# MLP weight sums by accumulating DMAs between DRAM tensors instead of on VectorE

## The chip, the cores and the metric

The kernel runs on one NeuronCore of a Trainium2 chip. Its engines are named as the profile names them: PE (TensorE matmuls), PEld (the weight loads of PE), DVE (VectorE), ACT (ScalarE), POOL (GpSimd) and SP (SyncE, which here only issues DMAs). POOL also issues some DMAs. Sixteen DMA engines move the data of all queues. The metric is the time of one execution on the device in microseconds (us); the kernel before takes 2281.39 us, the median of 3 runs (2279.77 to 2282.05).

## The reference

One layer of a hybrid encoder over 2048 prompt frames and 64 frames of a running stream, 2112 tokens of width 1024, all in float32:

```python
a = rmsnorm(h, norm1);  z = a @ w_in                     # one projection, 2816 columns
attn_o = windowed attention with sinks;  ret_o = chunkwise retention
h = h + concat(attn_o, gated_norm(ret_o)) @ w_out
u = relu(rmsnorm(h, norm2) @ w_up)                       # 1024 x 4096
h = h + (u * u) @ w_down                                 # 4096 x 1024
y = rmsnorm(h, norm_f)
```

The change concerns `w_up` and `w_down`. Every matrix product is made from operands split into a high and a low part, three passes on TensorE. The two products of the MLP are moreover made by a seven-product (Strassen-Winograd) form: each matrix is cut into 2 x 2 blocks, and of the weight blocks L11, L12, L21 and L22 four sums and differences S1 to S4 are needed besides three blocks that are used as they are. They are the same for all tokens, so they are made once and kept in DRAM.

## The kernel before

The program has two stretches. The **first** (to about 800 us) runs over 17 tiles of 128 tokens (the last one has 64) and over two halves of the heads, `ph` 0 and 1: 34 tiles, the first and last of each half in pairs. A tile has three groups, `ci` 0 to 2, of 24 matmuls with 384, 512 and 512 columns, which make the projection z (lines 526 to 529). Between these matmuls stand the small matmuls of attention and retention of the tiles before: scores `s`, transposes `pt`, products `po`, and for retention `ptr`, `pss`, `pr` and `pst`. Where they stand is set by a planner written in the kernel (lines 474 to 511: latencies in `LAT`, a clock that counts the z matmuls). The order on PE and SP is the order of the code (`manual_schedule`); on DVE, ACT and POOL a scheduler sets it. Each engine works in its order and waits at an instruction whose semaphores have not come.

A tile needs a load of x (`xr`, line 142, one buffer), a load of the rotary table (`rt`, line 160, two buffers, so it waits until the rotation before has read its table) and in `ph` 0 a load of the tokens for the norm (`xk`, line 163). They are issued on SP. ACT and POOL split x into `xh` and `xl` (lines 153 and 154). DVE makes the three products of a rotation (lines 193 to 195), POOL adds them into `zr` or `qk` (line 196). POOL also makes `es` (line 290), a small sum that ACT exponentiates (line 291) for the softmax sum, and issues the stores of the mixed heads (`mscr`, lines 332 and 417).

The sums S1 to S4 are made beside this, in 64 units of 128 x 1024 numbers, one per group: `sum_load` (line 567) issues two loads of 256 KB each into a buffer `sr`, `sum_make` (line 583) makes the four results on DVE in four instructions of 128 x 256 (lines 587 to 590), `sum_store` (line 593) stores them with one DMA of 512 KB to `uscr` (of `w_up`) or `sscr` (of `w_down`). Units 0 to 32 lie in `ph` 0 from its third tile on, units 33 to 63 in `ph` 1 from its third tile on; the change from one half to the other has none. Loads, sums and stores of different units overlap through the four buffers of the pool `wraw`, which the raw weights of the projection use too.

The **second** stretch makes the output projection and the MLP. It reads `uscr` and `sscr` again and again (`upr`, line 845; `dr`, line 928). `up_pair` (line 853) adds the seven products into four results, `right_sums` (line 694) makes the sums of the right-hand operand, and a long loop adds the products of `w_down` into the residual.

Of the kernel before, what the change touches and what calls it, by code (L numbers as in the profile page):

```python
# [11 lines left out]
F32 = mybir.dt.float32  # L12
F32R = mybir.dt.float32r
AF = mybir.ActivationFunctionType
ALU = mybir.AluOpType
# [14 lines left out]
NB = 352  # L30
# [9 lines left out]
def body(ctx, tc, xt, xtok, w1, wout, wup, wdn, gains, sinks, ck, cv, sret, rot, rdec, qdec, dmask,  # L40
         yT, nkp, nvp, nrp, nks, nvs, nrs):
    nc = tc.nc
# [52 lines left out]
    pp = ctx.enter_context(tc.tile_pool(name="pp", bufs=5, space=PS))  # L95

    tabs = {}

    def load_tables(ph):
        h = slice(2 * ph, 2 * ph + 2)  # L100
# [79 lines left out]
    def rotate(dst, z, T, t, nb, hd, cs):  # L180

        h = hd // 2
        r = rs[:T, t:t + 1]
        t1 = wk.tile([128, 512], F32, name="rot1", tag="rot1", bufs=2)[:T, :nb * hd].rearrange(
            "p (b d) -> p b d", d=hd)
        t2 = wk.tile([128, 512], F32, name="rot2", tag="rot2", bufs=2)[:T, :nb * hd].rearrange(
            "p (b d) -> p b d", d=hd)
        c, s = cs[:, 0], cs[:, 1]

        def bc(a, w):  # L190
            return a.unsqueeze(1).broadcast_to([T, nb, w])
# [3 lines left out]
        nc.vector.scalar_tensor_tensor(t2[:, :, h:], z[:, :, :h], r, bc(s[:, h:], h), op0=ALU.mult, op1=ALU.mult)  # L195
        nc.gpsimd.tensor_add(dst, t1, t2)

    def new_kw():
        return wk.tile([128, 2, 256], F32R, name="kw", bufs=2)
# [342 lines left out]
    S = NT - 1  # L542
# [8 lines left out]
    a, b = tiles[:2]  # L551
# [12 lines left out]
    ws[0, 2] = load_w(0, 2)  # L564
    raws = None

    def sum_load(u):

        w, j, h = u // 32, u % 32 // 2, u % 2
        r = wraw.tile([128, 4, 256], F32, name="sr", tag="raw")  # L570
        if w == 0:
            c = slice(h * 256, h * 256 + 256)
            src = [wup[e].rearrange("p (a c) -> p a c", a=2)[:, :, c] for e in (j, j + 16)]
            dst = uscr[:, j, :, c]
        else:
            d, c = j // 4, slice((j % 4 * 2 + h) * 256, (j % 4 * 2 + h) * 256 + 256)
            src = [wdn[e].rearrange("p (a f) n -> p a (f n)", a=2)[:, :, c] for e in (d, d + 4)]
            dst = sscr[:, d, :, c]
        for k in range(2):
            nc.sync.dma_start(r[:, 2 * k:2 * k + 2], src[k])  # L580
        return r, dst

    def sum_make(r, dst):

        s = wraw.tile([128, 4, 256], F32, name="st", tag="raw")
        L11, L12, L21, L22 = (r[:, k] for k in range(4))
        nc.vector.tensor_add(s[:, 0], L21, L22)
        nc.vector.tensor_sub(s[:, 2], L11, L21)
        nc.vector.tensor_sub(s[:, 1], s[:, 0], L11)
        nc.vector.tensor_sub(s[:, 3], L12, s[:, 1])  # L590
        return s, dst

    def sum_store(s, dst):
        nc.sync.dma_start(dst.rearrange("s p c -> p s c"), s)

    todo, loaded, made = list(range(64)), [], []
    first, change = groups.index((0, 2, 0)), groups.index((0, S - 2, 0)) - 3
# [31 lines left out]
    assert not todo and not loaded and not made  # L629
    while queue:  # L630
        run_ready(1e9)
    nc.sync.dma_start(nks[0:64], ck[64:128])
# [217 lines left out]
    def up_pair(p, j, after):  # L850
# [5 lines left out]
        for i in ORDER:  # L856
            w = wslot("wu")
            split(w[:, 0], w[:, 1], src[i])
            ah, al = A[p, i]
            o = bank[i][:, :NB]  # L860
            for k in range(4):
                wh, wl = (w[:, x, k * 128:k * 128 + 128] for x in range(2))
                nc.tensor.matmul(o, wh, ah[:, k], start=k == 0 and i in (1, 6, 5), stop=False, skip_group_check=True)  # L863
                nc.tensor.matmul(o, wh, al[:, k], start=False, stop=False, skip_group_check=True)  # L864
                nc.tensor.matmul(o, wl, ah[:, k], start=False, stop=k == 3 and i in (2, 4, 3), skip_group_check=True)  # L865
            if i == 1:
                nc.scalar.activation(pc, o, AF.Copy)
            elif i == 6:
                add(u2, o, pc)
            elif i == 7:  # L870
                add(u3, o, pc)
                add(C[:, 3], c[:, :NB], u3)
            elif i == 2:
                nc.scalar.activation(C[:, 0], o, AF.Copy)
            elif i == 4:
                add(C[:, 2], o, pc)
            elif i == 3:
                add(C[:, 1], o, u2)
            after(i)
        V = C[:, 0:4]  # L880
        nc.scalar.activation(V, V, AF.Relu)
# [133 lines left out]
    for n, (p, i, d) in enumerate(steps):  # L1015
# [21 lines left out]
        if i == 1:  # L1037
            nc.scalar.activation(x1, o, AF.Copy)
            add(h[11], h[11], x1)
        elif i == 2:  # L1040
            add(h[11], o, h[11])
            s1(h[11])
        elif i == 6:
            add(x1, o, x1)
        elif i == 7:
            add(u3, o, x1)
            add(h[21], h[21], u3)
            add(h[22], h[22], u3)
        elif i == 4:
            add(h[21], o, h[21])  # L1050
            s1(h[21])
        elif i == 5:
            add(h[22], o, h[22])
            add(x1, o, x1)
# [109 lines left out]
```

## Time and profile before

| | before |
|---|---|
| median of 3 runs | 2281.39 us |
| the profiled execution's own time | 2280.28 us |
| its span, from the first to the last instruction | 2278.5 us |
| mean granted TensorE clock | 0.990 |
| PE / PEld / DVE / ACT / POOL busy | 97% / 93% / 69% / 49% / 19% |
| chain that ended last | PE 81%, DMA 6%, DVE 5%, POOL 2%, issue 2%, SPq 1%, ACT 1% |
| HBM read / written | 377.64 MB / 135.99 MB |
| DMA issued by SP (queue q1) | 503.77 MB, 67.2% of 16 engines' span |
| DMA issued by POOL (queue q0) | 9.87 MB, 1.3% of 16 engines' span |

Busy PE time is the union of matmul records whose ends are modelled, so a high share does not say that PE runs at its peak. The chain of waits follows the work that ended last back to what released it; a share of it is time in which only that step could move the end. "SPq", "DVEq" and the like are the sequencers of the engines, that is, the issue of DMAs and waits on semaphores.

### The profile page before, as it was taken

To read this page: it belongs to the slowest core of one execution; us is meant where nothing else is said; L and a number is where in the kernel's file an instruction comes from. 1 tells how busy PE (TensorE), PEld (TensorE's weight loads), DVE (VectorE), ACT (ScalarE), POOL (GpSimd) and SP (SyncE) were. 2 spreads that over 40 slices of the span, in tenths; PEclk is the share of its full clock that TensorE was granted. 3 is DMA by queue.
4 is the path that set the end of the run, shared out by engine and by line. 5 is a ranking of instruction groups with operands and counts; after the bars stand their busy time and mean duration, and the time that the engine had idled before them with its cause. 6 is when DMAs were issued, how large, how long until landed. Compare 5 with 4: busy or idle time off the path is not lost.

```text
span 2278.5 us, 35972 instructions
## 1 busy us (share of the span) xinstructions
PE 2216.6 (97%) x13256; PEld 2112.0 (93%) x13256; DVE 1571.3 (69%) x2716; ACT 1112.8 (49%) x1982; POOL 425.4 (19%) x518
## 2 busy tenths in 40 slices
PE   7999999999999999999999999999999999999998
PEld 5788888887888799999999999999999999999998
DVE  5777767576655647788678768666666876687665
ACT  5344446343343542455565657555544454454452
POOL 5444444333333222200000000000000200120012
PEclk9999999999999899999999999999999999999999
DMA  6666754577732579669879869776966777677662
GB/s 203 183 208 207 216 152 136 149 183 170 192 99 77 196 233 319 220 219 361 278 267 353 281 234 322 239 238 236 328 228 227 278 282 242 228 270 275 235 212 79
DMA packets 296753, 515.94 MB, mean 226 GB/s; under 512 B 23376, under 2 KB 194576, under 8 KB 296576
## 3 DMA queue, kind: packets, MB, share of 16 engines
q1 hardware_dynamic: 292608, 503.77, 67.2%
q0 software_dynamic: 3968, 9.87, 1.3%
q8 instruction: 104, 1.70, 0.3%
q14 instruction: 73, 0.60, 0.1%
HBM read 377.64 MB, written 135.99 MB: 225 GB/s over the span
## 4 chain that ended last, share of the span: by engine, by line
PE 81%; DMA 6%; DVE 5%; POOL 2%; issue 2%; SPq 1%; ACT 1%; DVEq 0%; POOLq 0%; ACTq 0%
PE y L1033 10%; PE y L1034 10%; PE y L1032 9%; PE b L864 4%; PE b L865 4%; PE b L863 4%; PE z L526 4%; PE z L527 4%; PE z L529 4%; PE y L738 3%; PE y L739 3%; PE y L740 3%; PE a L864 3%; PE c L864 3%; PE a L865 3%; PE c L865 3%
## 5 line engine op out<-in xcount | busy, mean ns | idle before, releaser
L1033 PE MATMUL y<-vl,wd 128*128 128x352 f32 x1344 | 438.2, 326 | 0.0
L1034 PE MATMUL y<-vh,wd 128*128 128x352 f32 x1344 | 436.1, 324 | 1.3 <-DVE wd L663 1.3
L1032 PE MATMUL y<-vh,wd 128*128 128x352 f32 x1344 | 433.6, 323 | 2.8 <-ACT wd L662 2.8
L526 PE MATMUL z<-w,xh 128*128 128x512 f32 (+1 forms) x816 | 326.8, 400 | 7.1 <-ACT w L86 7.1
L527 PE MATMUL z<-w,xh 128*128 128x512 f32 (+1 forms) x816 | 310.8, 381 | 1.3 <-DVE w L87 1.3
L662 ACT ACTIVATE wd<-dr 128x1024 fp32r<-128x1024 f32 x168 | 177.1, 1056 | 259.0 <-PE y L1034 189.6
L983 POOL TENSOR_TENSOR acc<-acc,sq 128x352 f32<-128x352 f32 x41 | 72.5, 1768 | 1222.4 <-ACT sq L979 1222.4
L662 ACT ACTIVATE wu<-upr 128x512 fp32r<-128x512 f32 x336 | 209.1, 627 | 174.5 <-PE b L865 83.7
L529 PE MATMUL z<-w,xl 128*128 128x512 f32 (+1 forms) x768 | 288.9, 376 | 0.0
L663 DVE TENSOR_TENSOR wd<-dr,wd 128x1024 fp32r<-128x1024 f32 x168 | 209.2, 1247 | 110.9 <-ACT wd L662 108.2
L663 DVE TENSOR_TENSOR wu<-upr,wu 128x512 fp32r<-128x512 f32 x336 | 230.8, 693 | 69.6 <-ACT wu L662 55.4
L1032 PEld LDWEIGHTS y<-vh,wd 128*128 128x128 f32 x1344 | 254.7, 189 | 3.1 <-ACT wd L662 3.1
L1034 PEld LDWEIGHTS y<-vh,wd 128*128 128x128 f32 x1344 | 253.2, 188 | 1.6 <-DVE wd L663 1.6
L1033 PEld LDWEIGHTS y<-vl,wd 128*128 128x128 f32 x1344 | 252.8, 188 | 0.0
L864 PE MATMUL b<-al,wu 128*128 128x352 f32 x576 | 185.8, 323 | 0.0
L863 PE MATMUL b<-ah,wu 128*128 128x352 f32 x576 | 185.6, 322 | 0.0
L865 PE MATMUL b<-ah,wu 128*128 128x352 f32 x576 | 185.4, 323 | 0.0
L526 PEld LDWEIGHTS z<-w,xh 128*128 128x128 f32 x816 | 156.7, 192 | 25.5 <-ACT w L86 7.3
L527 PEld LDWEIGHTS z<-w,xh 128*128 128x128 f32 x816 | 156.5, 192 | 22.6 <-DVE w L87 4.6
L529 PEld LDWEIGHTS z<-w,xl 128*128 128x128 f32 x768 | 144.8, 189 | 23.1
L663 DVE TENSOR_TENSOR vl<-rv,vh 128x1408 fp32r<-128x1408 f32 x84 | 136.2, 1623 | 37.8 <-ACT vh L662 37.3
L662 ACT ACTIVATE vh<-rv 128x1408 fp32r<-128x1408 f32 x84 | 116.0, 1380 | 55.5 <-DMA rv<-vscr 35.2
(283 smaller groups left out, 4835.6 us busy)
## 6 DMA issues: line engine op xcount, KB each, us to landing
rv<-vscr SPq DMA_DIRECT2D x84, 704.0 KB, 5.4
vscr<-C SPq DMA_DIRECT2D x48, 1056.0 KB, 5.9
upr<-uscr SPq DMA_DIRECT2D x192, 256.0 KB, 5.2
dr<-sscr SPq DMA_DIRECT2D x96, 512.0 KB, 4.4
upr<-in_wup SPq DMA_DIRECT2D x144, 256.0 KB, 4.2
dr<-in_wdn SPq DMA_DIRECT2D x72, 512.0 KB, 4.9
sr<-in_wup SPq DMA_DIRECT2D x64, 256.0 KB, 5.5
uscr<-st SPq DMA_DIRECT2D x32, 512.0 KB, 5.5
```

Source lines behind the costliest of these rows:

```text
L526: nc.tensor.matmul(z[:, :n], xh[:, k], wh, start=k == 0, stop=False)
L527: nc.tensor.matmul(z[:, :n], xh[:, k], wl, start=False, stop=k == NK - 1 and xl is None)
L529: nc.tensor.matmul(z[:, :n], xl[:, k], wh, start=False, stop=k == NK - 1)
L662: nc.scalar.activation(h, x, AF.Copy)
L663: sub(l, x, h.bitcast(F32))
L863: nc.tensor.matmul(o, wh, ah[:, k], start=k == 0 and i in (1, 6, 5), stop=False, skip_group_check=True)
L864: nc.tensor.matmul(o, wh, al[:, k], start=False, stop=False, skip_group_check=True)
L865: nc.tensor.matmul(o, wl, ah[:, k], start=False, stop=k == 3 and i in (2, 4, 3), skip_group_check=True)
L983: nc.gpsimd.tensor_add(self.acc, self.acc, sq)
L1032: nc.tensor.matmul(o, wh, vh, start=f == 0, stop=False)
L1033: nc.tensor.matmul(o, wh, vl, start=False, stop=False)
L1034: nc.tensor.matmul(o, wl, vh, start=False, stop=f == 15)
```

## The change

The 64 units on DVE go, with their loads, their stores and their buffers. There are 16 units of 2 MB instead, 8 of `w_up` and 8 of `w_down`, whose blocks are 512 KB each, and each unit is made by eight DMAs from DRAM to DRAM in six steps:

| step | on SP: plain copies | on POOL: accumulating DMAs |
|---|---|---|
| 0 | S1 = L21, S3 = L11 | |
| 1 | | S1 += L22, S3 += L21 |
| 2 | S2 = S1 | |
| 3 | | S2 += L11 |
| 4 | S4 = S2 | |
| 5 | | S4 += L12 |

Each step waits for the one before. Step k of unit u stands behind group `first + 4u + 2k`, so steps of three units meet in one place: every fourth group four copies are issued on SP, and two groups later four accumulating DMAs on POOL. On POOL they are ordered behind the last rotation addition traced before them (`last_pool`). The sums differ in sign from those before (additions only), so `right_sums` and some additions behind the products of the MLP become subtractions and the other way round, of the same shapes and in the same number.

```diff
@@ rotate
-        nc.gpsimd.tensor_add(dst, t1, t2)
+        last_pool[0] = nc.gpsimd.tensor_add(dst, t1, t2)
@@ instead of sum_load, sum_make, sum_store
-        for k in range(2):
-            nc.sync.dma_start(r[:, 2 * k:2 * k + 2], src[k])
...
-        nc.vector.tensor_add(s[:, 0], L21, L22)
-        nc.vector.tensor_sub(s[:, 2], L11, L21)
-        nc.vector.tensor_sub(s[:, 1], s[:, 0], L11)
-        nc.vector.tensor_sub(s[:, 3], L12, s[:, 1])
...
-        nc.sync.dma_start(dst.rearrange("s p c -> p s c"), s)
+    def blocks(u):
+        if u < 8:
+            j = slice(2 * u, 2 * u + 2), slice(2 * u + 16, 2 * u + 18)
+            return [uscr[k, j[0]].rearrange("j p c -> p j c") for k in range(4)], \
+                [wup[e, :, c:c + 512].rearrange("j p c -> p j c") for e in j for c in (0, 512)]
+        d, c = (u - 8) // 2, (u - 8) % 2 * 1024
+        return [sscr[k, d, :, c:c + 1024] for k in range(4)], \
+            [wdn[e].rearrange("p f n -> p (f n)")[:, a + c:a + c + 1024] for e in (d, d + 4) for a in (0, 2048)]
+
+    def sum_step(u, k):
+        (S1, S2, S3, S4), (L11, L12, L21, L22) = blocks(u)
+        copies, sums = {0: ([(S1, L21), (S3, L11)], ()), 1: ((), [(S1, L22), (S3, L21)]), 2: ([(S2, S1)], ()),
+                        3: ((), [(S2, L11)]), 4: ([(S4, S2)], ()), 5: ((), [(S4, L12)])}[k]
+        for dst, src in copies:
+            nc.sync.dma_start(dst, src)
+        with tc.issue_after(last_pool[0].ins):
+            for dst, src in sums:
+                nc.gpsimd.dma_start(dst, src, accum_op=ALU.add, max_dma_last_dim=4096)
+
+    first = groups.index((0, 2, 0))
+    for u in range(16):
+        for k in range(6):
+            sums.setdefault(first + 4 * u + 2 * k, []).append((u, k))
@@ in the loop over groups
-        if made:
-            sum_store(*made.pop())
-        if todo and (first <= i < change or ph == 1 and t > 1):
-            loaded.append(sum_load(todo.pop(0)))
...
         group(ph, t, ci, n_)
-        if loaded and (len(loaded) > 1 or not todo or not first <= i < change - 1 and ph == 0):
-            made.append(sum_make(*loaded.pop(0)))
+        for x in sums.pop(i, ()):
+            sum_step(*x)
@@ right_sums, and likewise behind the products
-        sub(t[:, 0:2], r[:, 1::2], r[:, 0:2])
-        sub(t[:, 2], r[:, 3], t[:, 0])
+        sub(t[:, 0:2], r[:, 0:2], r[:, 1::2])
+        add(t[:, 2], r[:, 3], t[:, 0])
```

On SP, one tile of `ph` 1 before (xr is the load of x, rt that of the rotary table, sr the loads of a unit, sscr<-st its store):

```order
L142 DMA xr<-in_xt 128x8x128 [waits DMAHW5_49,Pool_49]
L594 DMA sscr<-st 128x4x256 [waits DMAHW6_49,DVE_49]
L580 DMA sr<-in_wdn 128x2x256 [waits DMAHW2_49]
L580 DMA sr<-in_wdn 128x2x256 [waits DMAHW0_49]
L160 DMA rt<-in_rot 128x384 [waits DMAHW1_49,DVE_49]
L594 DMA sscr<-st 128x4x256
L580 DMA sr<-in_wdn 128x2x256 [waits DMAHW4_49,DMAHW3_49]
L580 DMA sr<-in_wdn 128x2x256
L594 DMA sscr<-st 128x4x256 [waits DMAHW5_49,DVE_49]
L580 DMA sr<-in_wdn 128x2x256 [waits DMAHW6_49,DMAHW2_49]
L580 DMA sr<-in_wdn 128x2x256 [waits DMAHW7_49]
L142 DMA xr<-in_xt 128x8x128 [waits DMAHW0_49,Pool_49]
```

Between the two loads of x stood two or three units; a store there waits for DVE. The same queue now, likewise in `ph` 1 (sscr<-sscr are the copies S4 = S2 and S2 = S1, which wait for accumulating DMAs, the semaphores DMASW; sscr<-in_wdn are S1 = L21 and S3 = L11):

```order
L143 DMA xr<-in_xt 128x8x128 [waits DMAHW6_49,DMAHW0_49,Pool_49]
L161 DMA rt<-in_rot 128x384 [waits DMAHW7_49,DVE_49]
L585 DMA sscr<-sscr 128x1024 [waits DMASW1_49]
L585 DMA sscr<-sscr 128x1024 [waits DMAHW1_49,DMASW2_49]
L585 DMA sscr<-in_wdn 128x1024 [waits DMAHW2_49]
L585 DMA sscr<-in_wdn 128x1024 [waits DMAHW3_49]
L143 DMA xr<-in_xt 128x8x128 [waits DMAHW6_49,DMAHW4_49,Pool_49]
L161 DMA rt<-in_rot 128x384 [waits DMAHW5_49,DVE_49]
L143 DMA xr<-in_xt 128x8x128 [waits DMAHW4_49,Pool_49]
```

No DMA of SP waits for a sum on DVE any more; the copies come four at a time, and two of the four wait for POOL's DMAs. On POOL, a place in `ph` 1 now (qk is the rotation addition of line 196, now 197, es the small sum for the softmax, now line 291, xl the split of x):

```order
L197 TENSOR_TENSOR qk<-rot_5784,rot_5785 128x512 [waits DVE_49]
L588 DMA sscr<-in_wdn 128x1024 [waits DMAHW7_49,DMASW6_49]
L588 DMA sscr<-in_wdn 128x1024 [waits DMAHW0_49,DMASW7_49]
L588 DMA sscr<-in_wdn 128x1024 [waits DMAHW1_49,DMASW0_49]
L588 DMA sscr<-in_wdn 128x1024 [waits DMAHW2_49,DMASW1_49]
L291 TENSOR_TENSOR es<-sk,ngm 128x4 [waits DVE_49]
L155 TENSOR_TENSOR xl<-xr,xh 128x1024 [waits DMAHW4_49,PE_49,Activation_49]
```

The four L588 rows are new, each behind the copy that it adds to (DMAHW); before, es stood right behind qk. The rest of POOL's order is nearly the same, and so is PE's. The 64 of them stand in 18 bursts of one to four, twelve of them behind a qk (ten of three or four, two of one or two) and six behind a zr. DVE has 256 instructions fewer.

More of the change, by code (lines that the diff above doesn't have):

```diff
@@ L97, in body @@
     tabs = {}
+    last_pool = [None]
     def load_tables(ph):
@@ L565, in body @@
     raws = None
[L567 to L578, printed above, removed]
-        for k in range(2):
-            nc.sync.dma_start(r[:, 2 * k:2 * k + 2], src[k])
-        return r, dst
@@ L583, in sum_make @@
[L583 to L593, printed above, removed]
-        nc.sync.dma_start(dst.rearrange("s p c -> p s c"), s)
-    todo, loaded, made = list(range(64)), [], []
@@ L597, in body @@
-    first, change = groups.index((0, 2, 0)), groups.index((0, S - 2, 0)) - 3
+    def blocks(u):
[6 more added lines that the diff above has]
+            [wdn[e].rearrange("p f n -> p (f n)")[:, a + c:a + c + 1024] for e in (d, d + 4) for a in (0, 2048)]
@@ L598, in body @@
+    first = groups.index((0, 2, 0))
+    sums = {}
+    for u in range(16):
+        for k in range(6):
+            sums.setdefault(first + 4 * u + 2 * k, []).append((u, k))
     aux = []
@@ L628, in body @@
             raws = None
-    assert not todo and not loaded and not made
+    assert not sums
     while queue:
@@ L868, in up_pair @@
             elif i == 6:
-                add(u2, o, pc)
+                sub(u2, o, pc)
             elif i == 7:
-                add(u3, o, pc)
-                add(C[:, 3], c[:, :NB], u3)
+                sub(u3, o, pc)
+                sub(C[:, 3], u3, c[:, :NB])
             elif i == 2:
@@ L875, in up_pair @@
             elif i == 4:
-                add(C[:, 2], o, pc)
+                sub(C[:, 2], o, pc)
             elif i == 3:
-                add(C[:, 1], o, u2)
+                sub(C[:, 1], o, u2)
             after(i)
@@ L1043, in body @@
         elif i == 6:
-            add(x1, o, x1)
+            sub(x1, o, x1)
         elif i == 7:
@@ L1052, in body @@
         elif i == 5:
-            add(h[22], o, h[22])
-            add(x1, o, x1)
+            sub(h[22], h[22], o)
+            sub(x1, o, x1)
             add(h[12], h[12], x1)
```

## The prediction

> **What bounds the kernel now.** I read the page first, then busy time by stage, then the waits of the first stretch, then its chain of waits in order of time.
>
> ```profile
> span 2278.5 us, 35972 instructions
> PE 2216.6 (97%) x13256; PEld 2112.0 (93%) x13256; DVE 1571.3 (69%) x2716; ACT 1112.8 (49%) x1982; POOL 425.4 (19%) x518
> ```
>
> PE is busy nearly throughout, so only time in which PE waits can be won. By stage (the stretch, its length, then busy time of PE, PEld, DVE, ACT, POOL with instruction counts, granted clock, DMA share and GB/s):
>
> ```profile
> 57.20:323.50 266.30, 254.14 (x1428) 218.44 (x1427) 196.01 (x491) 113.52 (x353) 113.92 (x184) 1.00 0.64 198
> 323.50:428.80 105.30, 104.67 (x591) 91.91 (x590) 67.22 (x159) 55.85 (x155) 43.74 (x63) 1.00 0.39 120
> 428.80:659.40 230.60, 215.86 (x1202) 186.72 (x1202) 159.16 (x422) 86.83 (x278) 77.62 (x103) 0.99 0.70 181
> 659.40:722.40 63.00, 63.00 (x362) 55.47 (x361) 32.43 (x87) 26.03 (x82) 22.54 (x30) 1.00 0.16 43
> 800.00:2278.50 1478.50, 1463.58 (x9102) 1462.57 (x9100) 1036.83 (x1391) 757.84 (x945) 114.53 (x66) 0.99 0.75 257
> ```
>
> I cut where the retention scores pss start; there are four per tile, so their counts in the first three stages give the tiles:
>
> ```profile
> L370 PE MATMUL pss<-rqT,rkT x48: 270/275/377, 57.2 to 301.8; 128*128 128x128 f32 x48
> ...
> L370 PE MATMUL pss<-rqT,rkT x20: 270/275/377, 323.5 to 417.3; 128*128 128x128 f32 x20
> ...
> L370 PE MATMUL pss<-rqT,rkT x40: 270/275/377, 428.8 to 636.9; 128*128 128x128 f32 x40
> ```
>
> Stage one, with sums: 12 tiles in 266.3 us, 22.2 us each. Stage two, the change of head groups, nearly without sums: 5 in 105.3, 21.06. Stage three, with sums: 10 in 230.6, 23.06. Stage four, without sums and with PE busy for all of its 63.0 us: three tiles, 21.0. So 21.0 us is PE's own pace, and tiles with sums take 1.2 and 2.06 us more. The MLP (last row) has PE busy for 99% of its time.
>
> The waits of the first stretch, and a piece of the chain in stage three, say why:
>
> ```profile
> DVE st L587 <- DMA sr<-in_wdn: 35.0, 13, 4.7
> DVE st L587 <- DMA sr<-in_wup: 22.5, 10, 4.0
> ...
> PE pr L380 <- DVE sd L373: 7.9, 6, 1.5
> ```
>
> ```profile
> 564.91 6.29 DMA sr<-in_wdn
> ...
> 571.30 0.68 DVE st L587
> ...
> 572.31 0.35 DVE sd L373
> ...
> 572.79 0.46 PE pr L380 x2
> ...
> 585.75 0.40 DVE rot L195
> ...
> 586.17 0.35 SPq L160
> ...
> 587.09 0.55 SPq L580
> ...
> 587.69 6.12 DMA sr<-in_wdn
> ```
>
> It is a ring. DVE stands at the sums until their load lands; the retention mask sd is queued behind them, PE waits for it (1.5 us at a time), the tile ends later, the rotation reads its table later, SP's load of the table, which waits for that, is later, and the next sum load stands behind it. From 564.91 to 587.69 the ring takes 22.78 us; without the sums PE's 21.0 us would decide.
>
> **What the change removes.** These instructions on DVE, with their waits:
>
> ```profile
> L588 DVE TENSOR_TENSOR st<-sr 128x256 f32<-128x256 f32 x64 | 43.5, 680 | 0.0
> ...
> L587 DVE TENSOR_TENSOR st<-sr 128x256 f32<-128x256 f32 x64 | 39.3, 614 | 58.8 <-DMA sr<-in_wdn 35.0 <-DMA sr<-in_wup 22.5 <-issue 1.3
> ...
> L589 DVE TENSOR_TENSOR st<-st,sr 128x256 f32<-128x256 f32 x64 | 30.4, 474 | 0.0
> ...
> L590 DVE TENSOR_TENSOR st<-sr,st 128x256 f32<-128x256 f32 x64 | 29.2, 456 | 0.8
> ```
>
> 142 us of DVE and 58 us of its waiting, in a stretch where DVE isn't the bound (159 of 230 us busy). What counts is the ring: 266.3 - 12 x 21.0 = 14.3 us in stage one and 230.6 - 10 x 21.0 = 20.6 in stage three, 34.9 at most. At least, if only the waits that name sd were won, 7.9. The ring was seen closed in nearly every tile of stage three: I take 20 there. In stage one the tiles also carry the load of the tokens and the first weights: I take 11 of 14. **Gain 31.**
>
> **What the signs cost.** Additions become subtractions of the same shape and number; the four rows above are an addition and three subtractions, and their means don't sort by operation. They lie beside a PE that is busy for 99%. Nothing; if a subtraction were a tenth slower, DVE (1036.83 of 1478.5 us) would still cover it.
>
> **What it adds on POOL.** 64 accumulating DMAs in 18 bursts of up to four. No row shows one. The nearest are POOL's stores of 256 rows (mix) and of 128 rows (st):
>
> ```profile
> L332 POOL DMA_DIRECT2D mscr<-mix x34 | 25.8, 760 | 39.1 <-DVE mix L331 28.2 <-ACT qT L246 3.8 <-PE pss L370 3.2
> ...
> L404 POOL DMA_DIRECT2D out<-st x8 | 4.6, 575 | 9.3 <-DVE st L401 9.3
> ```
>
> The blocks of w_up have 256 rows, those of w_down 128: four take 3.0 or 2.3 us. From above: if each row needed twice the work, the slope between the rows (185 ns per 128 rows) gives 1.13 us each, 4.5 a burst. Nothing would be the lower end. What stands behind a burst, in a tile of stage four:
>
> ```profile
> 680.73 0.42 PE L526 MATMUL z<-w,xh 128*128 128x384 f32 x1
> ...
> 683.89 0.55 SPq L142 DMA_DIRECT2D xr<-in_xt  x1
> ...
> 689.01 0.87 POOL L196 TENSOR_TENSOR zr<-rot,rot 128x320 f32<-128x320 f32 x1 [2.79 <-DVE rot L195]
> ...
> 696.55 0.35 SPq L160 DMA_DIRECT2D rt<-in_rot  x1
> ...
> 696.61 1.29 POOL L196 TENSOR_TENSOR qk<-rot,rot 128x512 f32<-128x512 f32 x1 [4.35 <-DVE rot L195]
> 698.07 0.20 POOL L290 TENSOR_TENSOR es<-sk,ngm 128x4 f32<-128x4 f32 x1 [0.17 <-DVE ngm L284]
> ...
> 699.61 0.21 ACT L291 ACTIVATE es<-es 128x4 f32<-128x4 f32 x1
> 699.94 0.39 ACT L364 ACTIVATE rkT<-ptr 128x256 f32<-128x256 f32 x1
> ...
> 701.37 0.60 PE L370 MATMUL pss<-rqT,rkT 128*128 128x128 f32 x4
> ```
>
> Behind zr POOL has 6.7 us until qk: the six bursts there cost nothing. Behind qk comes es, ready at 698.27, which ACT takes at 699.61: 1.34 us of slack; ACT then copies rkT, done at 700.33, and PE's pss is at 701.37: 1.04 more. A burst of B us starts at 697.90, so es is late by about B, and PE by B - 2.4: 0.6 us at 3.0, nothing at 2.3, 2.1 at 4.5. Five or six of the ten large bursts behind qk are of w_up: 3 us; from above 10 x 2.1 = 21. I take **4**.
>
> **What it adds on the DMA engines.** Per burst 2 MB are copied and 2 MB accumulated. The rate follows from packets' time: the SP queue's rows (packets, MB, share of 16 engines' time) in the MLP, 900 to 2200 us, and in stage three; below them a store of POOL with its time to landing:
>
> ```profile
> q1 hardware_dynamic: 153792, 343.29, 76.6%
> ...
> q1 hardware_dynamic: 43885, 38.57, 65.6%
> ...
> mscr<-mix POOLq DMA_DIRECT2D x32, 128.0 KB, 2.3
> ```
>
> 343.29 MB in 0.766 x 16 x 1300 us is 21.5 GB/s per engine with rows of 1.4 to 5.6 KB, 345 GB/s for 16; stage three, with rows of mostly 1 KB, has 15.9 and 254. The new rows have 2 and 4 KB: 512 KB take 1.5 us (2.1 at the slower rate). An accumulate lies between one such pass (1.5) and three (read, read, write one after the other: 4.6); I take two, 3.05, in the middle. A burst's third accumulate, for which SP's copies wait, is then down about 0.8 + 3 x 3.05 + 2 = 12 us after the first issue (2 us of the store's 2.3, since its 128 KB move in 0.4); bounds 7.3 and 16.6. (The Trainium skill, Collectives: The Full Stack, section The bandwidth ceiling: the fold count and why AG ≠ RS ≠ AR, puts the cost of an add in the DMA engines at a second source read, so half a copy's rate: 3.05 us by it, and the sum stays; no row before shows an accumulate, so the trace can't agree yet.)
>
> Is 12 us late? Counted from a tile's start (680.73), POOL issues behind zr at 9.1 us or behind qk at 17.2, SP copies behind the load of x at 3.2 or behind that of the table at 15.8. Three bursts fill four tiles; between accumulate and next copies lie 19, 6.7 and 7.0 us, between copies and next accumulates 14, 14 and 22. SP may stand: the load of x at 683.89 is for the next tile, 21 us behind 680.73. POOL may not: after the 7.0 us gap the next accumulates come 21.0 us behind the former, less the copies' 8 us, so up to 13 us of landing are free, and 12 fits barely. At 16.6 POOL would stand 3.6 us in each of five rounds. I take **3** (0 to 18).
>
> The load of the tokens, issued behind the table, meets a burst in one of four tiles, and ACT waits for it already:
>
> ```profile
> ACT xk L164 <- DMA xk<-in_xtok: 18.0, 12, 3.3
> ```
>
> 1.5 us a tile now; doubled in three tiles of stage one, and with DMA engines busier in general, **4** (0 to 12). The weights of the second head group come through SP behind copies that were not there: five tiles at PE's pace show slack; **2** (0 to 6). On SP 128 DMAs fewer are issued; it wasn't the end of any long wait but in the ring: nothing.
>
> **Sum.** 2280.3 (this execution) - 31 + 4 + 3 + 4 + 2 = 2262; the median lies 1.1 us above the profiled one, within the bounds. With all costs at their lower ends and the whole ring won: 2245. With all at the upper ends (21, 18, 12, 6) and 31 won: 2306.
>
> **Rivals.** (1) POOL's burst eats the gain: an accumulating DMA takes 1.5 us of POOL, B is 6, PE loses 3.6 us ten times, and the time is about 2280, no change. For it: nothing of that kind was seen, and POOL stands in the chain. Against: 128 more rows cost only 0.19 us.
>
> (2) Slower: the accumulates land late. POOL works in order, and an accumulate whose copy hasn't landed stops es, zr and qk. Place: the 7.0 us gap, five rounds. Price: landing time less 13 us, each round, and from 21 us on in the next gap too. It decides from 13 + 18 / 5 = 17 us on, where the 18 us won are gone; at 25 us it is 5 x (12 + 4) = 80 us on top of 2259, about 2340. For it: three passes are 16.6 us already; with two passes a round of 28 us (four groups) holds 6.1 us of copies, 12.2 of accumulates and some 6 of the tiles' own transfers (x, tokens, table, mixed heads, 1.5 MB a tile), 87% of the DMA engines' time, against 0.64 and 0.70 now. Against: rows are longer than now, 2 and 4 KB for 1 KB.
>
> (3) The ring opens but the next one closes nearby: in stage one the load of table and tokens (SP waits for DVE's rotation, then ACT for the load) holds the tile at 22 us without any sum. Then only stage three is won: 2280 - 20 + 10 = 2270. Against: stage two's first tiles still load tokens and run at 21.06.
>
> **How the numbers follow.** A measurement of this kernel can tell about 0.2%, 4.6 us, from no change. My case 0.54, at 2262, its own range 2247 to 2274; (3) 0.14, 2270; (1) 0.12; (2) 0.20. Of (1) I count 0.08 as same and 0.04 as just faster; of (2) 0.02 as same. Faster 0.72, same 0.10, slower 0.18. The range 2247 to 2298 leaves out a tenth for a worse (2) and some for more than 31 won.
>
> **What would show it.** Right: no st on DVE, waits of DVE for sum loads gone, tiles of stage one and three at 21 to 21.6 us, POOL rows L588 near 0.6 to 0.8 us, landing of an accumulate below 13 us. Wrong by (1): L588 rows of 1.5 us and PE waiting for rkT or pt. Wrong by (2): POOL idle before L588 with a copy's landing as releaser, zr and qk late, PE waiting at pq and ptr. Wrong by (3): PE waits for ACT's zr or vs in stage one with no sum near. The MLP should be the same to within a few us; if it isn't, the signs or the DRAM layout matter after all.

## The result, and the profile after

The changed kernel takes 2349.83 us (median of 4 runs, 2346.35 to 2352.45), the kernel before 2281.72 us beside it: a ratio of 1.0299, 95% interval 1.0281 to 1.0316. It is slower by 3%, where 2262 us and a range of 2247 to 2298 were forecast.

The page of the changed kernel, the lines that answer to those shown of before and, of the parts on queues and chain, three more:

```profile
span 2350.7 us, 35610 instructions
PE 2241.2 (95%) x13256; PEld 2134.7 (91%) x13256; DVE 1469.8 (63%) x2460; ACT 1115.4 (47%) x1982; POOL 485.2 (21%) x582
...
q1 hardware_dynamic: 237312, 470.21, 59.5%
q0 software_dynamic: 17280, 43.43, 10.0%
...
PE 83%; DMA 8%; ACT 2%; DVE 2%; POOL 2%; issue 1%; SPq 1%; DVEq 0%; POOLq 0%; ACTq 0%
```

DVE is busy for 101 us less, yet DMA's share of the chain has grown from 6% to 8%. The same stretches of time as before (the columns are those of the prediction's rows; the tiles now lie later in them):

```profile
57.20:323.50 266.30, 229.36 (x1233) 199.14 (x1232) 118.33 (x308) 99.79 (x307) 126.24 (x189) 0.92 0.67 159
323.50:428.80 105.30, 93.65 (x494) 79.93 (x493) 52.54 (x129) 43.11 (x122) 47.60 (x66) 0.94 0.78 192
428.80:659.40 230.60, 206.91 (x1114) 180.25 (x1113) 112.81 (x284) 87.85 (x266) 98.28 (x127) 0.93 0.74 173
```

PE is busy for 529.9 of these 602.2 us, before for 574.7, and it does 2841 matmuls in them where it did 3221. Tiles without sums take 21.0 us still. Those with sums now repeat in fours in `ph` 0: from one pss to the next 33.4, 33.7, 24.0 and 21.0 us, then 31.9, 32.0, 24.0 and 21.5. From POOL's last es of the first stretch on, the two kernels keep the same pace; the whole loss lies ahead of it (1495 us from there to the end, 1496 before).

What waits there (45 to 860 us; waiting engine and line, what it waited for, us in total, times, longest):

```profile
SPq L585 <- DMA uscr<-in_wup: 172.4, 16, 25.4
SPq L585 <- DMA sscr<-in_wdn: 118.3, 14, 25.0
...
ACT xh L154 <- DMA xr<-in_xt: 58.0, 7, 11.7
...
ACT xk L165 <- DMA xk<-in_xtok: 21.3, 11, 6.8
PE pt L310 <- DVE p L299: 20.1, 8, 3.9
...
PE pq L245 <- DVE hl L231: 16.6, 3, 8.7
...
PE prt L415 <- DVE ro L407: 10.5, 3, 7.9
...
POOL sscr L588 <- DMA sscr<-in_wdn: 1.3, 1, 1.3
POOL sscr L588 <- DMA sscr<-sscr: 0.7, 1, 0.7
```

SP stood for 291 us at copies whose accumulate had not landed; POOL, which was to be the engine that stands, for 2 us. Late loads of x reach PE through ACT's xh: ahead of PE's two long waits at pq (8.7 and 7.0 us) ACT had just stood 11.1 and 9.4 us for x. SP's own timeline shows what is queued behind such a copy:

```profile
109.72 0.33 SPq L161 DMA_DIRECT2D rt<-in_rot  x1
110.11 0.42 SPq L164 DMA_DIRECT2D xk<-in_xtok  x1
133.07 3.40 SPq L585 DMA_DIRECT2D uscr<-uscr  x2
136.51 1.62 SPq L585 DMA_DIRECT2D uscr<-in_wup  x2
138.24 0.59 SPq L143 DMA_DIRECT2D xr<-in_xt  x1
138.88 1.44 SPq L161 DMA_DIRECT2D rt<-in_rot  x1
140.37 2.08 SPq L164 DMA_DIRECT2D xk<-in_xtok  x1
```

SP is ahead of the engines. It reached the copies at 110.5 us, 15 us before POOL issued their accumulates (at 125.7), and stood there until 133.07. The load of x, the table and the tokens then left within 2.1 us of each other, behind 2 MB of copies; xk landed 11.1 us after its issue.

A second thing happens on POOL and ACT (the engine's timeline, one burst):

```profile
167.52 4.76 POOL L588 DMA_DIRECT2D uscr<-in_wup  x4
170.41 2.10 POOL L291 TENSOR_TENSOR es<-sk,ngm 128x4 f32<-128x4 f32 x1
```

```profile
169.32 0.40 ACT L365 ACTIVATE rkT<-ptr 128x256 f32<-128x256 f32 x1
170.44 1.06 ACT L154 ACTIVATE xh<-xr 128x1024 fp32r<-128x1024 f32 x1 [0.73 <-PE z L528]
171.41 0.61 ACT L347 ACTIVATE vs<-z,rsv 128x128 f32<-128x128 f32 x2
171.91 0.47 ACT L352 ACTIVATE sig<-z,hrs 128x256 f32<-128x256 f32 x1
172.55 0.20 ACT L292 ACTIVATE es<-es 128x4 f32<-128x4 f32 x1 [0.17 <-POOL es L291]
...
176.57 0.60 ACT L313 ACTIVATE ph<-pt 128x512 fp32r<-128x512 f32 x1 [3.81 <-PE pt L310]
```

The burst of four takes 4.76 us of POOL, and es is done at 172.5, 4.8 us after its inputs. ACT also has another order than before: es stood right behind the exponentials of p, ahead of rkT, in the tiles of this kind, and now, in seven tiles whose burst lies ahead of es on POOL, it stands behind all that follows: the square of the tokens xk, the split xh, and vs and sig, which scale retention's values and make its gate. ACT's order in two successive tiles of the changed kernel, both in `ph` 0, with what lies between left out:

```
L288 ACTIVATE p,sm<-s,ngm 128x192 x4
L365 ACTIVATE rkT<-ptr 128x256
L165 ACTIVATE xk,ss<-xk 128x1024
L154 ACTIVATE xh<-xr 128x1024
L347 ACTIVATE vs<-z,rsv 128x128 x2
L352 ACTIVATE sig<-z,hrs 128x256
L292 ACTIVATE es<-es 128x4
...
L288 ACTIVATE p,sm<-s,ngm 128x192 x4
L292 ACTIVATE es<-es 128x4
L365 ACTIVATE rkT<-ptr 128x256
L165 ACTIVATE xk,ss<-xk 128x1024
```

Presumably the scheduler that orders ACT saw es late, behind POOL's burst, and put other work first, among it the square of the tokens (xk), which waits for a DMA. The softmax sum on DVE, the scaled p and PE's transposes pt follow from es, so that all these now delay PE. In the burst shown, POOL is the later of the two: ACT was through with the rest and stood 0.17 us for es. In the other six tiles of this kind es lay ready 1.4 to 3.4 us before ACT came to it. A wait of ACT for the tokens themselves lies ahead of es in one of the seven tiles (0.7 us); in `free_copies` and `plain_pool` below it does in five tiles, 0.3 to 1.4 us each.

### The profile page after: what moved, and what is told of

Same layout as the page of the kernel before. It is cut to its first block, busy times and chain, and to the rows that moved or that the text cites. A ratio compares the mean times of both kernels' runs of the same rounds, so it can differ in the third digit from the quotient of the medians.

```text
span 2350.7 us, 35610 instructions
## 1 busy us (share of the span) xinstructions
PE 2241.2 (95%) x13256; PEld 2134.7 (91%) x13256; DVE 1469.8 (63%) x2460; ACT 1115.4 (47%) x1982; POOL 485.2 (21%) x582
## 4 chain that ended last, share of the span: by engine, by line
PE 83%; DMA 8%; ACT 2%; DVE 2%; POOL 2%; issue 1%; SPq 1%; DVEq 0%; POOLq 0%; ACTq 0%
PE y L1026 9%; PE y L1027 9%; PE y L1025 9%; PE z L527 5%; PE z L528 5%; PE z L530 4%; PE b L856 4%; PE b L857 4%; PE b L858 4%; DMA xk<-in_xtok 3%; PE y L731 3%; PE y L732 3%; PE c L856 3%; PE a L856 3%; PE a L857 3%; PE y L733 3%
## 5 line engine op out<-in xcount | busy, mean ns | idle before, releaser
L527 PE MATMUL z<-w,xh 128*128 128x512 f32 (+1 forms) x816 | 333.7, 409 | 12.3 <-ACT w L86 7.5
L528 PE MATMUL z<-w,xh 128*128 128x512 f32 (+1 forms) x816 | 316.2, 387 | 1.3 <-DVE w L87 1.3
L530 PE MATMUL z<-w,xl 128*128 128x512 f32 (+1 forms) x768 | 293.9, 383 | 1.6 <-POOL xl L155 1.6
L527 PEld LDWEIGHTS z<-w,xh 128*128 128x128 f32 x816 | 161.0, 197 | 31.7 <-ACT w L86 7.9
L528 PEld LDWEIGHTS z<-w,xh 128*128 128x128 f32 x816 | 160.5, 197 | 23.2 <-DVE w L87 4.9
```

The costliest lines, as they stand in the source:

```text
L527: nc.tensor.matmul(z[:, :n], xh[:, k], wh, start=k == 0, stop=False)
L528: nc.tensor.matmul(z[:, :n], xh[:, k], wl, start=False, stop=k == NK - 1 and xl is None)
L530: nc.tensor.matmul(z[:, :n], xl[:, k], wh, start=False, stop=k == NK - 1)
```

## Experiments

Three causes were on the table: SP stands at copies (theory 1, later B); POOL's burst makes es late (theory 2, later A, with ACT's order as part of it); the traffic itself slows loads (theory 3, later C). All times below are medians, the ratio is to the kernel before on the same chip.

| run | us | ratio, 95% interval |
|---|---|---|
| changed kernel | 2349.8 | 1.0299, 1.0281 to 1.0316 |
| `no_sums` | 2244.5 | 0.9844, 0.9828 to 0.9860 |
| `copies_only` | 2246.7 | 0.9848, 0.9832 to 0.9864 |
| `far_copies` | 2312.3 | 1.0141, 1.0125 to 1.0158 |
| `free_copies` | 2313.3 | 1.0145, 1.0122 to 1.0168 |
| `es_first` | 2307.7 | 1.0116, 1.0088 to 1.0143 |
| `free_es` | 2286.3 | 1.0027, 1.0011 to 1.0043 |
| `plain_pool` | 2289.7 | 1.0044, 1.0027 to 1.0061 |
| `spread` | 2273.4 | 0.9969, 0.9956 to 0.9982 |
| `spread_plain` | 2256.1 | 0.9896, 0.9880 to 0.9913 |
| `mixed` | 2251.6 | 0.9875, 0.9857 to 0.9894 |
| `signs` | 2278.8 | 0.9993, 0.9980 to 1.0007 |
| `dve_late` | 2288.8 | 1.0042, 1.0027 to 1.0057 |

**The floor, and the copies.** `no_sums` drops the calls of `sum_step`, and the MLP reads raw blocks where it read sums:

> Left out: all copies and all accumulating DMAs; the MLP reads raw weight blocks (of the same shape and number of loads) where it read S1 to S4. This is the floor under every theory of the loss. By the prediction's step on the gain (34.9 us at most) it takes 2245 to 2250 us, with the sum-free tiles' 21.0 us in every stretch of the first stage and a granted clock of 0.99 or more there. If it stays above 2265 us, the gain of 31 us was never there to be had, and the loss is smaller than it seems. The difference to the changed kernel's 2350 us, some 100 us, is what the remaining runs have to divide.

`copies_only` has the loop of `free_copies` (below) without its accumulates:

```diff
-            for dst, src in sums:
-                nc.gpsimd.dma_start(dst, src, accum_op=ALU.add, max_dma_last_dim=4096)
+            pass
```

> Left out: the accumulating DMAs. The 64 copies of 512 KB stay on SP in the changed kernel's places, all of weight blocks, so that none waits; ACT has es right behind p. Theory A (order of es, from POOL's bursts): 2244 to 2254 us. Theory C (traffic): the copies ahead of the loads in SP's queue slow them, 2265 us or more; if it is the accumulates' traffic alone that slows them, it can't be seen here.

2244.5 and 2246.7 us: the gain that was forecast was there to be had (PE's tiles take 21.0 us in both), and 64 copies on SP that wait for nothing cost 2 us. The other 103 us of the changed kernel come with the accumulates.

**SP's waits.** Two edits that leave bytes and bursts as they are, but take away what the copies wait for; `far_copies` moves a unit's later steps back for it, `free_copies` leaves every place:

```diff
 far_copies
-            sums.setdefault(first + 4 * u + 2 * k, []).append((u, k))
+            sums.setdefault(first + 4 * u + (0, 2, 8, 10, 16, 18)[k], []).append((u, k))
 free_copies
-                        ... 2: ([(S2, S1)], ()), 3: ((), [(S2, L11)]), 4: ([(S4, S2)], ()), 5: ((), [(S4, L12)])
+                        ... 2: ([(S2, L11)], ()), 3: ((), [(S2, S1)]), 4: ([(S4, L12)], ()), 5: ((), [(S4, S2)])
```

> Same copies, same accumulating DMAs, same bursts (four copies, then two groups later four accumulates), but a copy that reads an accumulated block stands six groups behind the accumulate in the code instead of two. Theory 1 (SP runs ahead, stands at such a copy until the accumulate has landed, and the loads of x, table and tokens behind it are late): the idle time of SP at line 585 before a landed accumulate falls from 291 us to under 30 us, and the time falls from 2350 us to 2255 to 2290 us. Theory 2 (POOL's issue of a burst, 4.7 us, which makes es late) and theory 3 (the traffic of the copies and accumulates slows the loads): bursts and bytes are the same, so 2330 us or more.

> Same places, same bytes, but S2 is first a copy of L11 and S4 a copy of L12, and the accumulates add S1 to S2 and S2 to S4. The copies on SP so wait for no accumulate; the accumulate on POOL waits for the one before it, four groups earlier. Theory 1 (SP stands): as with the copies further behind, 2255 to 2290 us, and no idle time of SP before a landed accumulate. Theories 2 and 3 (burst on POOL, traffic): 2330 us or more, since the order on SP, POOL and PE and the bytes are the same as in the changed kernel. If it is much slower than the run with the copies further behind, the wait has moved to POOL.

Both come out at the same, 2312 and 2313 us: SP's waits are worth 37 us, and no theory had that number; 1 had expected 60 us or more, 2 and 3 at most 20. The waits of `far_copies`, where of SP's 291 us one row is left, and xh waits for x once:

```profile
SPq L585 <- DMA sscr<-in_wdn: 4.5, 2, 3.5
...
ACT xk L165 <- DMA xk<-in_xtok: 25.8, 13, 6.1
PE pt L310 <- DVE p L299: 26.5, 8, 4.9
...
ACT xh L154 <- DMA xr<-in_xt: 9.3, 1, 9.3
```

PE's wait at pq has gone from 16.6 us to 1.6. What is left is PE's wait at pt, which has grown, and ACT's wait for tokens.

**The place of the burst on POOL.** The burst is ordered behind es instead of behind the rotation, once with SP's waits and once without:

```diff
-        last_pool[0] = nc.gpsimd.tensor_add(dst, t1, t2)
+        nc.gpsimd.tensor_add(dst, t1, t2)
...
-        nc.gpsimd.tensor_add(es[:, :nu], sk[:, g, :nu], ngm[:, :nu])
+        last_pool[0] = nc.gpsimd.tensor_add(es[:, :nu], sk[:, g, :nu], ngm[:, :nu])
```

> The changed kernel, with one thing moved: its accumulating DMAs are ordered on POOL behind the last es traced, not behind the last rotation. In the order of the changed kernel the scheduler has put the exponential es of ACT behind the square of the tokens xk, xh, vs and sig in the tiles with a burst; here it stands right behind the exponentials of p again, as without sums. SP still stands at the copies that wait for accumulates. Theory A (order of es: PE's transposes pt wait through es for the load of tokens, so every late load costs PE time): the waits of PE at pt go, and the time falls from 2350 us to 2265 to 2305 us, though SP stands as long as before. Theory B (SP's standing costs by itself, through late x): above 2330 us. Theory C (traffic): above 2330 us.

> Both: copies that wait for no accumulate, and bursts behind es. With free copies alone it took 2313 us, 69 us above the 2244 us without sums; there two of four tiles (27.9 and 26.3 us) have es behind the square of the tokens, one (28.5 us) a load of tokens of 9.7 us, one takes 21.0 us. Theory A (order of es): the first two go to 21 to 22 us, 11 of 18.7 us in four tiles, so 2262 to 2280 us. Theory C (traffic of 33.5 MB of copies and 33.5 MB of accumulates slows the load of tokens): above 2295 us.

| | burst ahead of es | burst behind es | |
|---|---|---|---|
| copies wait for accumulates | 2349.8 | 2307.7 | -42 |
| copies wait for nothing | 2313.3 | 2286.3 | -27 |
| | -37 | -21 | -64 together |

Each repair takes a good part, and the two overlap by 15 us; why they overlap is not shown. PE's wait at pt is gone in `es_first` (no row of it, 20.1 us before), while SP still stands 141 us. But a part of it has only moved, to PE's wait at pr, which was 6.2 us in the changed kernel:

```profile
PE pr L381 <- ACT vs L347: 34.6, 7, 10.9
```

The products pr need vs, and vs stands on ACT behind xk and xh. Ahead of the longest of these waits ACT had stood 12.8 us for the tokens. So a late load holds PE whatever the place of es; it takes another way. `es_first` came out 3 us above what theory A expected, and `free_es` above its 2262 to 2280: 40 us over `copies_only` remain with both repairs. In `free_es` PE still waits 10.5 us at pr, and 8.1 us once at pq, with ACT 10.4 us at the weights of the second head group (w1raw) just before.

The other side of it, the burst ahead of es without adding, without copies and without SP's waits:

```diff
-        for dst, src in copies:
-            nc.sync.dma_start(dst, src)
...
-                nc.gpsimd.dma_start(dst, src, accum_op=ALU.add, max_dma_last_dim=4096)
+                nc.gpsimd.dma_start(dst, src, max_dma_last_dim=4096)
```

> Left out: the copies on SP and the adding. The 64 DMAs on POOL stay in the changed kernel's places and bursts, behind the rotation, as plain copies of the same blocks; ACT's order is that of the changed kernel, with es behind the square of the tokens, xh, vs and sig in the tiles with a burst. SP never stands and there is half the traffic of copies and a quarter of that of the accumulates. Theory A (the order of es costs by itself, since even with a load of tokens that lands in 3.7 us PE stood 3.2 us at pt and ran 2 us slower behind it): six to eight tiles of 26 to 27 us, 2270 to 2290 us, against 2247 us of the run with copies on SP alone. Theory E (the order costs only where late loads meet it): tiles of 21 to 22 us, 2248 to 2260 us.

2289.7 us, 43 us over `copies_only`: the burst and the order behind it cost about that much without adding and without SP's waits, though a burst of four plain DMAs takes POOL 2.8 us and not 4.76. In the seven tiles where PE waits, es is done on POOL 2.2 to 2.9 us after its inputs (0.3 without a burst), and ACT takes it after 5.2 to 6.5 us (1.6 without), each time right behind sig. So of some 4.3 us of delay POOL's 2.6 us, less ACT's slack of 1.3 us, explain a third; the rest comes from ACT's order. That is read from the delays: no run has the burst ahead of es with ACT's order of before. PE's row is much like that of the changed kernel:

```profile
PE pt L310 <- DVE p L299: 24.0, 7, 4.8
```

**The time of the accumulates on the DMA engines.** `spread` has copies as in `free_copies`, one per group, and accumulates one per group, ordered behind the power rr, as far ahead of the next load of tokens as POOL's order allows; `spread_plain` is the same with the adding dropped, as in `plain_pool`:

```diff
-            sums.setdefault(first + 4 * u + 2 * k, []).append((u, k))
+            sums.setdefault(first + 4 * u + (0, 1, 2, 3, 5, 6, 11, 16)[k], []).append((u, k))
...
-        nc.gpsimd.tensor_tensor(rr[:T], s2[:T], mhalf[:T], op=ALU.pow)
+        last_pool[0] = nc.gpsimd.tensor_tensor(rr[:T], s2[:T], mhalf[:T], op=ALU.pow)
```

> Copies that wait for no accumulate, one per group of matmuls; accumulates one per group too, ordered behind rr (the power of the norm of retention), after which POOL has 2.8 us idle and then 4.3 us behind the stores of the mixed heads, and some 10 us ahead of the next load of tokens. ACT has es right behind p. Theory A with the collisions taken away: 2246 to 2262 us, faster than the kernel before by 20 us or more. If the traffic itself slows the first stage wherever it lies (theory C): above 2275 us.

> Left out: the adding. The kernel with copies and accumulates spread (2273 us) with its 64 accumulating DMAs made plain copies on POOL, of the same blocks, in the same places, with the same waits. There a packet of 2048 B takes 178 ns of a DMA engine as an accumulate and 84 ns as a copy, the DMA engines are 99% busy from an accumulate's issue until the next load of tokens, and this load lands in 6.8 us instead of 3.9, so that ACT stands 3.2 us per tile. Theory C (the accumulates' time on the DMA engines is what is left): the packets fall to 84 to 90 ns, the load of tokens lands in under 5 us, and the time falls to 2246 to 2258 us. Theory D (POOL's issue, 1.2 us each, is what is left): 2268 us or more, since POOL issues as many DMAs as before.

`spread` is 0.3% faster than the kernel before, but 27 us above `copies_only`, between what theories A and C expected. DMA engines in 210 to 300 us of it, in 40 slices (tenths), and the two queues:

```profile
DMA  0799999993008999999600499999991039999999
...
q0 software_dynamic: 3648, 7.34, 45.4%
q1 hardware_dynamic: 8403, 11.15, 35.8%
```

POOL's queue moves two thirds of SP's bytes there and takes more of the engines' time. The DMA engines are full for 16 to 18 us of each tile of 23, and the load of tokens meets them full here too. The tile xk from 57 to 420 us, first in `spread`, then in `copies_only`:

```profile
  DMA xk<-in_xtok: 31.5, 13
...
DMA to landing us min/median/max: 3.8/6.6/8.0
```

```profile
  DMA xk<-in_xtok: 8.9, 13
...
DMA to landing us min/median/max: 3.7/3.9/4.7
```

PE meets this at pr, which needs vs behind xk; `copies_only` has no such row:

```profile
PE pr L381 <- ACT vs L347: 19.7, 9, 5.1
```

Single packets in the changed kernel's DMA records (2 KB from 57 to 300 us, where the blocks are w_up's, 4 KB from 300 to 700 us):

```
                      2048 B copy   2048 B accumulate   4096 B copy   4096 B accumulate
median ns of one           84             178                159              328
```

Without the adding (`spread_plain`) it takes 2256.1 us: the adding is 17 of the 27 us, with POOL issuing as many DMAs as before. POOL's time is not held fixed by this, since three plain DMAs of w_up take it 2.2 us and three accumulates 3.6. What speaks for the DMA engines is the way to PE: the load of tokens lands in 4.6 us, ACT's wait for it falls from 31.5 to 14.7 us and PE's at pr from 19.7 to 2.4. Some 9 us go with the plain DMAs of POOL that stay.

**A version that beats both.** If it is the load of tokens that suffers, the second half of the heads, which has none, should take more of the sums:

```diff
+    second = groups.index((1, 2, 0))
     for u in range(16):
-        for k, g in enumerate((0, 1, 2, 3, 5, 6, 11, 16)):
-            sums.setdefault(first + 4 * u + g, []).append((u, k))
+        for k in range(8):
+            g = first + 6 * u + (0, 3, 7, 10, 2, 5, 9, 12)[k] if u < 6 else \
+                second + 4 * (u - 6) + (0, 1, 2, 3, 2, 3, 5, 8)[k]
+            sums.setdefault(g, []).append((u, k))
```

> As the spread kernel, but two accumulates per tile instead of three while the tiles load tokens (the first half of the heads), and the rest in the second half of the heads, whose tiles have no such load, though there they come three per tile over all of its tiles. Theory C (accumulates collide with the load of tokens): most of the 29 us that the spread kernel has above the kernel without sums goes, 2250 to 2264 us. If every accumulate costs the same wherever it lies: 2270 to 2277 us as spread.

2251.6 us, 1.25% faster than the kernel before and 98 us faster than the changed one, with the same bytes and as many DMAs. ACT's wait for the tokens falls from the 31.5 us of `spread` to 12.9, their landing from 6.6 to 4.1 us, and PE's wait at pr is gone. Its stages:

```profile
57.20:323.50 266.30, 264.07 (x1508) 231.10 (x1507) 141.16 (x375) 121.55 (x373) 141.19 (x216) 1.00 0.63 160
323.50:428.80 105.30, 104.28 (x586) 91.25 (x585) 68.47 (x164) 53.25 (x154) 47.93 (x61) 1.00 0.52 147
428.80:659.40 230.60, 229.63 (x1319) 202.27 (x1318) 120.64 (x319) 96.30 (x300) 113.66 (x145) 1.00 0.82 193
```

PE is busy for 598.0 of 602.2 us, with the DMA engines at 0.82 in the third row, above the changed kernel's 0.67 to 0.78 in these stages. Total traffic was not the bound; it cost where it met a load that ACT waits for.

**Signs, and the ring of the kernel before.** `signs` is the kernel before with the signs of the change. `dve_late` is that one with its sums in place, a unit so needing one buffer for two, and made one group later (the units of the first half of the heads are loaded one group sooner at its end):

```diff
-        s = wraw.tile([128, 4, 256], F32, name="st", tag="raw")
-        L11, L12, L21, L22 = (r[:, k] for k in range(4))
...
+        L21, L22, L11, L12 = (r[:, k] for k in range(4))
+        nc.vector.tensor_add(L11, L11, L21)
+        nc.vector.tensor_add(L21, L21, L22)
+        nc.vector.tensor_add(L22, L11, L22)
+        nc.vector.tensor_add(L12, L22, L12)
...
-        if loaded and (len(loaded) > 1 or not todo or
+        if loaded and (len(loaded) > 2 or not todo or
```

> The kernel before with the signs of the change alone: the sums are made on DVE as before, by four additions, and the additions behind the MLP's products are changed as in the change. By the prediction (signs cost nothing) 2281 us within 4 us. If the signs had a price of their own in the MLP, it would show here, and the 2350 us would be part of it.

> Not DMAs: the sums on DVE as in the kernel before, with the signs of the change, made in place (four additions whose results take the buffers of their operands), so that a unit needs one buffer instead of two, and its sums are made one group of matmuls later. In the kernel before a load of a unit lands in 6.3 us, and DVE stands for it 1.5 us per group with sd behind; here it has some 7 us more. If that ring (load, sums, sd, pr, rotation, table, next load) is what the 35 us between the kernel before and the kernel without sums are, it opens: 2246 to 2262 us, with tiles of 21 to 21.5 us. If it is DVE's own work for the sums or the traffic: 2272 us or more.

Signs cost nothing that can be measured. `dve_late` came out slower, not faster: 2288.8 us, 0.4% above the kernel before and in the range that was expected if the ring were not the cause. SP's timeline in it, one tile:

```profile
600.05 0.35 SPq L161 DMA_DIRECT2D rt<-in_rot  x1
600.44 0.43 SPq L594 DMA_DIRECT2D sscr<-sr  x1
600.98 1.54 SPq L581 DMA_DIRECT2D sr<-in_wdn  x2
602.56 0.61 SPq L594 DMA_DIRECT2D sscr<-sr  x1
606.57 1.20 SPq L581 DMA_DIRECT2D sr<-in_wdn  x2
608.38 0.54 SPq L143 DMA_DIRECT2D xr<-in_xt  x1
```

SP had stood at the table since 590.2 us, for DVE's rotation, with stores and loads of units queued behind it; when it goes on, they go out together, and in the chain of waits DVE's sums follow the landing of the first of them, 5.9 us later. So here too a ring closes through SP's wait at rt, though the sums are made a group later. The edit also made another wait larger: with the sums in place, a load into a buffer waits for the store out of it, 63.5 us in 27 waits of SP against 4.0 in 3 in the kernel before. `dve_late` so neither opens the ring nor proves it; that putting the loads of the units ahead of rt would open it is a guess from this timeline and was not tried.

## Why the prediction was wrong

**The gain was right in size.** 31 us were forecast, from PE's 21.0 us per tile; `no_sums` shows 37, a little above the 34.9 put as the most, `copies_only` 34 and `mixed` 28. That the ring was what held these tiles is not shown apart, since `dve_late` did not open it. Signs: nothing, as put. An accumulate's time on the DMA engines, put at 3.05 us for 512 KB as two passes: 256 packets of 178 ns or 128 of 328 ns on 16 engines are 2.85 and 2.62 us by their medians. The rule of the Trainium skill cited there (Collectives: The Full Stack, section The bandwidth ceiling: the fold count and why AG ≠ RS ≠ AR: an add needs a second source read) agrees with the records: 2.06 to 2.12 times a copy's packet. That a second read is the reason, no record shows. The landing, put at 12 us for a burst's third (7.3 to 16.6), was near: in the 15 bursts of three or four the third was down 12.3 to 16.9 us after the first issue, 13.2 in the middle.

**"SP may stand" was the step that failed first.** The landing term (3 us, at most 18) asked only whether POOL would stand, and it doesn't. SP was let off because the load of x behind the copies is for the next tile. But SP runs ahead of PE, so that it reaches a copy before the accumulate is even issued and stands up to 25 us, more than the 21 us allowed; and two more loads stand behind it that are due sooner, table and tokens. Measured: 37 us (21 with es first). Rival (2) had this mechanism on the wrong engine: its 2340 us is near the result by chance, since its place (POOL at the gap of 7.0 us) shows 2 us of waiting.

**The burst term (4 us, at most 21) was missized by its parts.** Four w_up accumulates take 4.76 us of POOL, not 3.0 (the upper end had 4.5); by the prediction's own formula, B - 2.4, that is 2.4 us a burst. The rest was not in the formula. The order on ACT had changed, and the prediction looked only at the orders of SP, POOL and PE: in seven tiles with a burst es went behind xk, xh, vs and sig. And PE pays a second time for a wait, as told below. Measured: 42 us (27 with free copies).

**The load of tokens (4 us, at most 12)** was counted in one of four tiles. With bursts behind es and no waits on SP 40 us are left over `copies_only`, from late loads among them; how they divide between tokens, table, weights of the second head group and POOL's issue was not separated by a run. With the accumulates spread out, the adding costs 17 us, and PE's wait at pr, behind the tokens, is as much longer with it. The share of 87% of the DMA engines that was written under rival (2) belonged here.

The upper ends of all terms were added to 2306 us, so the range could not hold the result: the landing and the burst came to twice their own bounds, and the 17 us of the adding in `spread` already pass the 12 of the tokens. Rival (3) didn't come about: without sums the tiles take 21.0 us. Rival (1) named the right resource and its sign was seen (PE waiting at pt). Its 36 us, 3.6 in each of ten bursts, is near the measured 42 by chance: it came from bursts of 6 us, and bursts of 4.76 us did it together with ACT's order.

## What to carry to other kernels

An engine that only issues DMAs stands like any other: a DMA that waits for another DMA belongs in a queue in which nothing behind it is due within its worst landing, and the distance has to be counted from where that queue runs ahead to, not from where the code stands. An operation put ahead of a short one on one engine can change the order that a scheduler gives a second engine, so the orders of all engines that follow must be compared, not only of those that were edited. Work moved to DMA engines is free only where no load with a waiting reader falls into its time: here the same bytes cost 103 us or 5 over the copies alone, by their places, their order and what they wait for.

## What the runs showed of the hardware

PE is slower after it has waited. The granted clock (the number behind the counts) in two pieces of the changed kernel, a stretch of 140 us and 6 us in it right behind a wait of 7.9 us:

```profile
110.00:250.00 140.00, 120.73 (x648) 104.56 (x647) 63.18 (x162) 52.43 (x161) 65.11 (x93) 0.93 0.65 148
...
157.00:163.00 6.00, 5.67 (x19) 4.67 (x20) 1.43 (x4) 1.81 (x5) 1.59 (x2) 0.52 0.08 25
```

PE's busy time per matmul in the first three stages is 529.9 us / 2841 = 187 ns, before 574.7 / 3221 = 178; over 2841 matmuls that is some 23 us of slower work beside 72 us of waiting. A wait of PE so cost about a third as much again, which no term of the prediction held. The Trainium skill (TensorE: Matmul & The Clock Gate, section Part 1: The HAM clock gate (the "warmup" mystery)) gives half the clock after an idle window of about 3.4 us; the trace agrees with 0.52 behind this wait. But a wait need not be that long: behind two waits of 2.5 us (at 285 and 620 us) the clock was 0.50 over the next 3.3 us.

An accumulating DMA from DRAM to DRAM takes 1.2 us of POOL with 256 rows and 0.9 us with 128 in a burst. The same DMAs without adding, in `plain_pool`, take 0.70 and 0.53, near POOL's stores of mix and st (0.76 and 0.58).
